# A hybrid decoder layer on one core: attention pieces a group later, psw in float32r, wider matmuls at the head of up, the last normalisation on VectorE

## The chip, the cores and the metric

The kernel runs on one core of one Trainium2 chip. The metric is the device time of one execution in microseconds (us). The core's engines are TensorE (PE in the profile, with its weight loads as PEld), VectorE (DVE), ScalarE (ACT), GpSimd (POOL) and SyncE (SP), which issues the large DMAs.

## The reference

One layer of a hybrid decoder for 256 tokens of width 1024, in float32. The functions below are cut to what is computed.

```python
def hybrid_mixer(x, w_in, ...):
    proj = x @ w_in + b_in          # q_m k_m v_m o_m i_m f_m  q_b k_b v_b  g_a g_b
    q_m, k_m = split(silu(causal_dwconv(concat(q_m, k_m), conv_qk)))      # 4 taps
    h_m = mlstm_chunkwise(q_m, k_m, v_m, i_m, f_m)       # 4 heads x 256, stabilised by a running maximum
    y_a = sigmoid(o_m) * head_norm(h_m, mlstm_norm)
    y_b = moba_attention(q_b, k_b, v_b, rel_bias)        # 8 heads x 128; 256 tokens are one block: causal softmax + T5 bias
    merged = sigmoid(g_a) * (y_a @ w_branch_a) + sigmoid(g_b) * (y_b @ w_branch_b)
    return merged @ w_out

def conv_gated_mlp(x, w_up, conv_ffn, w_down):
    g, up = split(causal_dwconv(x @ w_up, conv_ffn))     # 3 taps, 2 x 2816 columns
    return (silu(g) * up) @ w_down

x = layer_norm(ALPHA * x + hybrid_mixer(x, ...), ln1_g, ln1_b)
x = layer_norm(ALPHA * x + conv_gated_mlp(x, ...), ln2_g, ln2_b)
```

## The kernel before, in words

All weights arrive as a stream of 81 chunks, each 128 partitions x 2048 float32 columns (1 MB). `chunk_order` fixes their order: four chunks o; four groups of qm, qb, km, kb, vm, vb, ga, gb; then wa and wb in turn, wo, up, and dn between the rest of up. One chunk is one step `s` of the main loop in `run`. A step emits, in this order, the element work that is due (`elem_work`, which also splits the weights of chunk s+2), the load of chunk s+5, the chunk's own matmuls (`step_...`), and then the small matmuls that hang on this step (`side_pe`). Nothing reorders this: each engine carries out its instructions as written, and waits on semaphores for the others.

Products are made in float32r from two parts. A value is split into a high part (a float32r copy, on ScalarE) and a low part (value minus copy, on VectorE); `mm3` adds high x high, high x low and low x high in three matmuls. Line 91 is the copy and 92 the subtraction of every split; lines 125, 126 and 127 are the three matmuls of every `mm3`. Some small products are made in plain float32 instead: the profile shows each as two records.

For each group g, whose first step is b (`start_g[g]`), `group_schedule` hangs the two branches on the steps b to b+8. The names in the rows are: psw, a row of the running maximum spread over all partitions (from nM); pss, the scores of the mLSTM head; psl, the logits of the two attention heads; wt, exponential weights made from psw (`el_w`); sph and spl, the parts of the weighted scores (`el_s`, `el_s2`); psn, the mLSTM output; lg, the softmax in place; pst, its transposes; pth, ptl and ptf, their parts (`el_t`); psy, the transposes of the normalised mLSTM output yt; pso, the attention output; yah, yal, ybh, ybl, the parts of both branches' outputs (`el_y`, `el_o`). `mixed[s]` sets the order of the pieces within the element work of a step. Side results lie in five PSUM banks (`ps_side`) and chunk results in three (`ps_main`); a new tile takes a bank that an older one has left, and waits until that has been read.

The first two up chunks run one half of the tokens at a time with tokens as rows, since the second half of x1 (the first layer norm's output) comes later; `ps_t` are the transposes of x1, and `aheadh`, `aheadl` the split weights of these chunks. The other up chunks give features as rows, and `up_evac` convolves and gates them into hh and hl, the left operands of dn. dn accumulates all 1024 columns of both token halves in five banks (ffn).

After the last matmul, `finish` adds the residual (`ln_part`: r, then statistics bs), aggregates them (`ln_scale`: mv, then rs = (variance + EPS) to the power -0.5 on GpSimd), and `ln2_out` normalises r and stores it. In the second token half the columns 768 to 1023 go through ScalarE and GpSimd, the others in pieces of 256 through VectorE.

Of the kernel before, what the change touches and what calls it, by code (L numbers as in the profile page):

```python
# [18 lines left out]
P = 128  # L19
# [50 lines left out]
class Kernel:  # L70
# [101 lines left out]
    def run(self):  # L172
# [75 lines left out]
        self.xfirst = mp.tile([P, P + 16], F32R, name="xfirst")[:, 16:]  # L248
# [34 lines left out]
        self.nM = mp.tile([P, S], F32, name="nM")  # L283
        g.memset(self.nM, 0.0)
# [18 lines left out]

        self.rel_bias_expand(rel, onehot)
# [13 lines left out]
        for s, (kind, i) in enumerate(self.order):  # L318
# [12 lines left out]
            if s == first["wo"]:  # L331
                self.elem_work(s)
                y_cm.__exit__(None, None, None)
                zp = ahead_cm.__enter__()
                for j in range(2):
                    self.extra[first["up"] + j] = tuple(
                        zp.tile([P, 2112], F32R, name=f"ahead{n}{j}")[:, 8:8 + 2048] for n in "hl")
# [5 lines left out]
            self.elem_work(s, [] if late or s == 8 else self.split_parts(s + 2))  # L343
            self.load(s + 5)
# [192 lines left out]
    def gates_schedule(self, bif):  # L537
# [66 lines left out]
    def group_schedule(self, g):  # L604
# [5 lines left out]
        def pe_m():  # L610

            psw = self.ps_side([P, S], f"psw{g}")
            nc.tensor.matmul(psw, self.ident[:, g:g + 1].to_broadcast([P, P]), self.nM, start=True, stop=True)
            st["psw"] = psw

        def pe_s():
            qh, ql = self.hl["qm"]
            kh, kl = self.hl["km"]
            pss = self.ps_side([P, 2, S], f"pss{g}")

            for k in range(2):
                nc.tensor.matmul(pss[:, 0, P:], self.cv["km"][:, k, P:], self.cv["qm"][:, k, P:],
                                 start=k == 0, stop=k == 1)
            for k in range(2):
                self.mm3(pss[:, 1, :], kh[:, k, 0:P], kl[:, k, 0:P], qh[:, k, :], ql[:, k, :], k == 0, k == 1)
            st["pss"] = pss
# [89 lines left out]
        def pe_l(i):  # L716
            qh, ql, qf = self.qb
            kh, kl = self.hl["kb"]
            ps = self.ps_side([P, 2, S], f"psl{g}_{i}")

            nc.tensor.matmul(ps[:, 0, 0:P], qf[:, i, :], self.kbf[:, i, :], start=True, stop=True)
            self.mm3(ps[:, 1, :], qh[:, i, :], ql[:, i, :], kh[:, i, :], kl[:, i, :], True, True)
            st["l", i] = ps

# [38 lines left out]
        def pe_o():  # L763
            ps = self.ps_side([P, 2, S], f"pso{g}")
            vh, vl, vf = self.vb
            for i in range(2):
                th, tl, tf = self.pt[i]
# [312 lines left out]
    def ln2_out(self, t):  # L1080
# [18 lines left out]
        if t == 1:  # L1099
            store(768, D)  # L1100
# [89 lines left out]
```

## Time and profile before

| | us |
|---|---|
| median of 3 runs | 490.73 (490.67 to 490.86) |
| the profiled execution's own time | 490.16 |
| its span | 488.4 |
| TensorE busy | 477.0 (98%) |
| VectorE busy | 369.3 (76%) |
| ScalarE busy | 286.2 (59%) |
| GpSimd busy | 30.6 (6%) |

The mean granted clock of TensorE was 0.994. Times in rows count from the span's start. A row of the timeline gives the start, the duration, the engine, the line, the operation, the output and inputs by their names, shapes, and how many equal instructions it merges; in brackets stands how long the engine was idle before it, and what ended that.

### The profile page before, as it was taken

The page shows a single profiled execution, that of the slowest core. Times are in us where ns is not written, and L with a number is a line of the kernel's source. Part 1 is how long each engine was busy: PE and PEld are TensorE (multiplying, and loading weights), DVE is VectorE, ACT ScalarE, POOL GpSimd, SP SyncE. Part 2 cuts the span into 40 slices and gives each one's busy share as a digit, 9 for nine tenths or more (in the row PEclk, how much of TensorE's full clock was granted, in tenths as well). Part 3 has the DMA queues.
Part 4 walks back from the last instruction along what each step waited for, and adds up shares of the span by engine and source line. Part 5 has one row for each costly group of instructions (what it writes and reads, how often), then busy time and mean ns, then how long its engine had stood idle before and what let it go on. Part 6 is the DMA issues. An engine that isn't in the chain of part 4 may idle for free.

```text
span 488.4 us, 9811 instructions
## 1 busy us (share of the span) xinstructions
PE 477.0 (98%) x4070; PEld 470.0 (96%) x4070; DVE 369.3 (76%) x659; ACT 286.2 (59%) x476; POOL 30.6 (6%) x46
## 2 busy tenths in 40 slices
PE   8999999999999999999999999999999999999992
PEld 4999999999999999999999999999999999999992
DVE  4967995788588858886677788988668766876886
ACT  5857767495658666856655622767456545654620
POOL 0600011001100110001000001000000000000001
PEclk9999999999999999999999999999999999999997
DMA  8984565555555645543964491827465556454202
GB/s 281 376 299 122 210 196 205 178 180 188 181 191 174 189 160 197 201 150 116 368 231 172 174 344 42 302 89 258 173 236 165 205 173 224 176 204 173 87 2 86
DMA packets 17886, 93.77 MB, mean 192 GB/s; under 512 B 4497, under 2 KB 4889, under 8 KB 7857
## 3 DMA queue, kind: packets, MB, share of 16 engines
q1 hardware_dynamic: 13682, 87.08, 50.1%
q0 software_dynamic: 4160, 6.07, 4.1%
q8 instruction: 32, 0.52, 0.4%
q14 instruction: 12, 0.10, 0.1%
HBM read 92.05 MB, written 2.63 MB: 194 GB/s over the span
## 4 chain that ended last, share of the span: by engine, by line
PE 97%; DMA 1%; DVE 1%; SPq 0%; ACT 0%; issue 0%; POOL 0%; POOLq 0%
PE ps_up L127 8%; PE ps_up L125 8%; PE ps_up L126 8%; PE ffn L127 4%; PE ffn L126 4%; PE ffn L125 4%; PE ps_vm L125 2%; PE ps_qm L125 2%; PE ps_vm L126 2%; PE ps_vm L127 2%; PE ps_ga L125 2%; PE ps_ga L127 2%; PE ps_vb L125 2%; PE ps_vb L126 2%; PE ps_vb L127 2%; PE ps_ga L126 2%
## 5 line engine op out<-in xcount | busy, mean ns | idle before, releaser
L92 DVE TENSOR_TENSOR wl<-raw,wh 128x1024 fp32r<-128x1024 f32 (+1 forms) x162 | 187.7, 1199 | 25.3 <-ACT wh L91 25.2
L91 ACT CAST wh<-raw 128x1024 fp32r<-128x1024 f32 (+1 forms) x162 | 158.4, 1030 | 8.6 <-DMA raw<-in_wst_dram 5.9
L127 PE MATMUL ps_up<-x1h,wl 128*128 128x256 f32 x320 | 88.5, 277 | 0.0
L126 PE MATMUL ps_up<-x1l,wh 128*128 128x256 f32 x320 | 88.5, 276 | 0.0
L125 PE MATMUL ps_up<-x1h,wh 128*128 128x256 f32 x319 | 88.3, 277 | 0.0
L126 PEld LDWEIGHTS ps_up<-x1l,wh 128*128 128x128 f32 x320 | 60.2, 188 | 0.0
L127 PEld LDWEIGHTS ps_up<-x1h,wl 128*128 128x128 f32 x320 | 60.1, 188 | 0.0
L125 PEld LDWEIGHTS ps_up<-x1h,wh 128*128 128x128 f32 x319 | 59.9, 188 | 0.0
L1020 DVE SCALAR_TENSOR_TENSOR cu<-ps_up,vec,cu 128x255 f32<-128x255 f32 (+1 forms) x80 | 33.1, 476 | 23.1 <-ACT cu L1016 23.0
L127 PE MATMUL ffn<-wh,hl 128*128 128x256 f32 (+1 forms) x170 | 47.7, 281 | 0.0
L126 PE MATMUL ffn<-wl,hh 128*128 128x256 f32 (+1 forms) x170 | 47.7, 281 | 0.0
L125 PE MATMUL ffn<-wh,hh 128*128 128x256 f32 (+1 forms) x170 | 47.7, 281 | 0.0
L91 ACT CAST hh<-cu 128x256 fp32r<-128x256 f32 x22 | 8.9, 407 | 42.9 <-DVE cu L1028 42.9
L126 PEld LDWEIGHTS ffn<-wl,hh 128*128 128x128 f32 x170 | 32.0, 188 | 0.3
L125 PEld LDWEIGHTS ffn<-wh,hh 128*128 128x128 f32 x170 | 31.9, 188 | 0.3
L127 PEld LDWEIGHTS ffn<-wh,hl 128*128 128x128 f32 x170 | 31.9, 188 | 0.3
L1016 ACT ACTIVATE cu<-ps_up,vec 128x256 f32<-128x256 f32 x40 | 16.7, 469 | 25.7 <-PE ps_up L127 25.7
L125 PE MATMUL ps_gb<-xth,wh 128*128 128x256 f32 x64 | 18.0, 282 | 0.0
L126 PE MATMUL ps_vm<-wl,xth 128*128 128x256 f32 x64 | 17.9, 280 | 0.0
L127 PE MATMUL ps_vm<-wh,xtl 128*128 128x256 f32 x64 | 17.9, 280 | 0.0
L927 POOL TENSOR_TENSOR rs<-rs,mhalf 128x1 f32<-128x1 f32 x4 | 2.7, 666 | 242.4 <-DVE rs L926 242.4
L125 PE MATMUL mix<-wh,mgh 128*128 128x256 f32 x64 | 17.8, 279 | 0.0
(295 smaller groups left out, 1441.7 us busy)
## 6 DMA issues: line engine op xcount, KB each, us to landing
raw<-in_wst_dram SPq DMA_DIRECT2D x78, 1024.0 KB, 4.9
raw<-in_wst_dram SPq DMA_DIRECT2D x5, 512.0 KB, 8.0
lnrow<-in_rows_dram POOLq DMA_DIRECT2D x4, 512.0 KB, 6.8
band<-table POOLq DMA_DIRECT2D x4, 384.0 KB, 12.2
toe<-band POOLq DMA_DIRECT2D x4, 256.0 KB, 4.4
xtok<-in_x_dram POOLq DMA_DIRECT2D x1, 1024.0 KB, 7.7
out_dram<-r SPq DMA_DIRECT2D x3, 256.0 KB, 2.0
raw<-in_wst_dram SPq DMA_DIRECT2D x2, 256.0 KB, 3.8
```

Of the source, the lines that this page charges most:

```text
L91: self.nc.scalar.copy(wh, raw)
L92: self.nc.vector.tensor_sub(wl, raw, wh.bitcast(F32))
L125: mm(ps, ah if first is None else first, bh, start=start, stop=False)
L126: mm(ps, ah, bl, start=False, stop=False)
L127: mm(ps, al, bh, start=False, stop=stop)
L927: nc.gpsimd.tensor_tensor(st["rs"], st["rs"], self.mhalf[:, 0:1], op=ALU.pow)
L1016: act.activation(cu[:, j, :], ps[:, j, :], AF.Copy, scale=tap(2, j))
L1020: v.scalar_tensor_tensor(cu[:, j, o:], ps[:, j, :S - o], tap(t, j), cu[:, j, o:], op0=ALU.mult, op1=ALU.add)
```

## The change

- `psw` is made from nM as float32r: rows 0 to 3 hold the high part, rows 32 to 35 the low part, and a 0/1 matrix `pick` adds both in one matmul.
- Scores and logits of a group form one piece, `pe_scores`, behind step b+4, in which all plain float32 products stand together. For groups 0 to 2, `pe_t` and `pe_y` move to step b+11 and `pe_o` into the next group's `pe_scores`; `el_t` and `el_y` follow at the head of step b+12's element work, `el_o` in step b+13. `el_w` of groups 1 to 3 moves from step b+5 to the end of step b+4's element work, and their psw one step earlier.
- In group 3, `pe_o` stands ahead of `pe_y`, and `el_y` first in the element work of step b+8. The split of the chunk after wa 0 and the load of three chunks later move from step b+7 to behind that element work.
- The first two up chunks are multiplied as 512 columns (both chunks beside each other in one pair of tiles, one bank for each token half).
- dn opens with eight matmuls of 512 columns where there were nine in each of its two outer products, and inside a product both column halves follow each other for each of the three parts.
- EPS is added to the first part's statistics. `ln2_out` is one product of 1024 columns and two of 512 on VectorE, with two stores for each token half; GpSimd and ScalarE no longer take part in it, but for the power.

TensorE around the scores of group 1, before (vm is the chunk ahead, vb the one behind):

```order
L127 MATMUL ps_vm_1342<-wh_1192,xtl 128x256
L613 MATMUL psw_1392<-nM,ident 128x256
L622 MATMUL pss_1394<-cvqm,cvkm 128x128 x2
L125 MATMUL pss_1394<-qmh,kmh 128x256
...
L127 MATMUL pss_1394<-qmh,kml 128x256
L721 MATMUL psl_0_1403<-kbf,qbf 128x128
L125 MATMUL psl_0_1403<-kbh,qbh 128x256
L126 MATMUL psl_0_1403<-kbl,qbh 128x256
L127 MATMUL psl_0_1403<-kbh,qbl 128x256
L125 MATMUL ps_vb_1439<-wh_1255,xth 128x256
```

And after, from the end of kb; pst_0_1297, pst_1_1301, psy_1305 and both pso belong to group 0:

```order
L127 MATMUL ps_kb_1246<-xth,wl_1092 128x256
L622 MATMUL psw_1295<-nM,xfirst 128x256
L763 MATMUL pst_0_1297<-ident,lg_793 128x128 x3
L763 MATMUL pst_1_1301<-ident,lg_880 128x128 x3
L723 MATMUL psy_1305<-ident,yt_891 128x128 x4
L125 MATMUL ps_vm_1338<-wh_1159,xfirst 128x256
...
L781 MATMUL pso_1_1392<-pth_710,vbl 128x256
L783 MATMUL pso_0_1391<-ptf_709,vbf 128x128
L783 MATMUL pso_1_1392<-ptf_712,vbf 128x128
L635 MATMUL pss_1388<-cvqm,cvkm 128x128 x2
L637 MATMUL psl_0_1389<-kbf,qbf 128x128
L637 MATMUL psl_1_1390<-kbf,qbf 128x128
```

The transposes of the group before now stand ahead of vm, and its pso opens the block behind vm, whose float32 products follow each other.

ScalarE in the element work of that step, before:

```order
L91 CAST kmh<-cvkm 128x512
L466 ACTIVATE kbh<-ps_kb_1279,vec 128x256 x2
L468 ACTIVATE kbf<-ps_kb_1279,vec 128x128 x2
L91 CAST wh_1328<-raw_1141 128x1024 x2
L631 ACT_TABLE_LOAD
L631 ACTIVATE wt_1411<-psw_1392,gcol 128x128
```

And after:

```order
L91 CAST kmh<-cvkm 128x512
L91 CAST pth_707<-pst_0_1297 128x256
L770 COPY ptf_709<-pst_0_1297 128x128
L91 CAST pth_710<-pst_1_1301 128x256
L770 COPY ptf_712<-pst_1_1301 128x128
L730 ACTIVATE yah<-psy_1305,vec 128x256 x2
L472 ACTIVATE kbh<-ps_kb_1246,vec 128x256 x2
L474 ACTIVATE kbf<-ps_kb_1246,vec 128x128 x2
L649 ACT_TABLE_LOAD
L649 ACTIVATE wt_1328<-psw_1295,gcol 128x128
L650 ACTIVATE wt_1328<-psw_1295,gcol 128x256
L91 CAST wh_1310<-raw_1108 128x1024 x2
```

Six pieces of the group before stand ahead of kb's evacuation, and the exponentials of psw stand ahead of the casts of the next weights.

VectorE at the end of the program, before:

```order
L925 BN_AGGR mv_1_4070<-bs_1_4069 128x2
L926 TENSOR_SCALAR rs_1_4071<-mv_1_4070 128x1
L1091 TENSOR_SCALAR nmr<-mv_1_4070,rs_1_4071 128x1
L932 SCALAR_TENSOR_TENSOR r_1_4068<-r_1_4068,mv_1_4070,lnrow_4262 128x256 x2
L935 SCALAR_TENSOR_TENSOR r_1_4068<-r_1_4068,rs_1_4071,lnrow_4264 128x256 x2
L932 SCALAR_TENSOR_TENSOR r_1_4068<-r_1_4068,mv_1_4070,lnrow_4262 128x256
L935 SCALAR_TENSOR_TENSOR r_1_4068<-r_1_4068,rs_1_4071,lnrow_4264 128x256
```

And after:

```order
L950 BN_AGGR mv_1_4027<-bs_1_4026 128x2
L1116 SCALAR_TENSOR_TENSOR r_1_4025<-r_1_4025,mv_1_4027,lnrow_4220 128x1024
L1119 SCALAR_TENSOR_TENSOR r_1_4025<-r_1_4025,rs_1_4028,lnrow_4222 128x512 x2
```

The two small instructions are gone, and all 1024 columns are on VectorE, in three instructions.

The core of the diff; of the schedule tables only the lines that move pieces are shown:

```diff
-            v.tensor_scalar(self.nM[0:4, :], M, -1.0, None, op0=ALU.mult)
+            v.tensor_scalar(nM, M, -1.0, None, op0=ALU.mult)
+            nc.scalar.copy(self.nM[0:4, :], nM)
+            v.tensor_add(self.pick, self.ident[:, 0:4], self.ident[:, 32:36])
+            v.tensor_sub(self.nM[32:36, :], nM, self.nM[0:4, :].bitcast(F32))
...
-            nc.tensor.matmul(psw, self.ident[:, g:g + 1].to_broadcast([P, P]), self.nM, start=True, stop=True)
+            nc.tensor.matmul(psw, self.pick[:, g:g + 1].to_broadcast([P, P]), self.nM, start=True, stop=True)
...
+        def pe_scores():
+            pss = st["pss"] = self.ps_side([P, 2, S], f"pss{g}")
+            psl = [self.ps_side([P, 2, S], f"psl{g}_{i}") for i in range(2)]
+            if g:
+                self.grp[g - 1]["out"]()
             for k in range(2):
+                mm(pss[:, 0, P:], self.cv["km"][:, k, P:], self.cv["qm"][:, k, P:], start=k == 0, stop=k == 1)
+            for i in range(2):
+                mm(psl[i][:, 0, 0:P], self.qb[2][:, i, :], self.kbf[:, i, :], start=True, stop=True)
             for k in range(2):
                 self.mm3(pss[:, 1, :], kh[:, k, 0:P], kl[:, k, 0:P], qh[:, k, :], ql[:, k, :], k == 0, k == 1)
+            for i in range(2):
+                self.mm3(psl[i][:, 1, :], bh[:, i, :], bl[:, i, :], ch[:, i, :], cl[:, i, :], True, True)
...
+            self.mixed[b + 4] = lambda w: prev["early"] + w + [el_w]
+        self.mixed[b + 5] = lambda w: [w[0]] + ([] if g else [el_w]) + [
...
+        for i in range(2):
+            at(self.side_pe, 6 if last else 11, lambda i=i: pe_t(i))
+        if last:
+            at(self.side_pe, 7, pe_o)
+        at(self.side_pe, 7 if last else 11, pe_y)
...
+            self.mixed[b + 8] = lambda w: [el_y] + w
...
+            st["early"] = [lambda: el_t(0), lambda: el_t(1), el_y]
+            at(self.side_elem, 13, el_o)
...
             if s == first["wa"]:
                 self.elem_work(s)
+                self.split(s + 1)
+                self.load(s + 4)
...
+        if st["n"] == 0:
+            m2 = st["bs"][:, 0, 2:3]
+            v.tensor_scalar(m2, m2, D * EPS, None, op0=ALU.add)
...
-                for j in range(2):
-                    self.mm_tok(self.w[s - i + j], [self.pt_up[j][:, t, :] for t in range(2)], self.x1h, self.x1l,
-                                toks=(i,), ks=(k,))
+                self.mm3(self.pt_up[i], self.x1h[:, k, c], self.x1l[:, k, c], wh[:, :, k, :], wl[:, :, k, :], k == 0,
+                         k == KT - 1)
...
-            n = cols[1] - cols[0] if k in (0, NF - 1) else 256
+            full = ((a, b),)
+            parts = [[(c, c + 256) for c in range(a, b, 256)]] * 3
+            if k == 0:
+                parts = [full, full, parts[2] if t else full]
+            elif k == NF - 1:
+                parts = [parts[0] if t else full, full, full]
+            for i, (left, right) in enumerate(((hh, wh), (hh, wl), (hl, wh))):
+                for lo, hi in parts[i]:
+                    self.nc.tensor.matmul(ps[:, lo - a:hi - a], left, right[:, lo:hi], start=k == i == 0,
...
+        v.scalar_tensor_tensor(r, r, mv[:, 0:1], gain, op0=ALU.subtract, op1=ALU.mult)
         for h in range(2):
-            cols = [slice(x, x + 256) for x in range(h * 512, 1024 if t == 0 and h else 768 if h else 512, 256)]
-            self.ln_apply(r, st, cols)
-            store(cols[0].start, cols[-1].stop)
-        if t == 1:
-            store(768, D)
+            c = slice(h * 512, h * 512 + 512)
+            v.scalar_tensor_tensor(r[:, c], r[:, c], rs, bias[:, c], op0=ALU.mult, op1=ALU.add)
+            nc.sync.dma_start(self.out[0, t * P:(t + 1) * P, c], r[:, c])
```

More of the change, by code (lines that the diff above doesn't have):

```diff
@@ L334, in run @@
                 zp = ahead_cm.__enter__()
+                self.pair = [zp.tile([P, 4160], F32R, name="ahead" + n)[:, 24:24 + 4096] for n in "hl"]
                 for j in range(2):
-                    self.extra[first["up"] + j] = tuple(
-                        zp.tile([P, 2112], F32R, name=f"ahead{n}{j}")[:, 8:8 + 2048] for n in "hl")
+                    self.extra[first["up"] + j] = tuple(t[:, j * 2048:(j + 1) * 2048] for t in self.pair)
             if s == first["up"]:
@@ L342, in run @@
             late = s == first["up"]
-            self.elem_work(s, [] if late or s == 8 else self.split_parts(s + 2))
-            self.load(s + 5)
+            before_wa = s == first["wa"] - 1
+            self.elem_work(s, [] if late or before_wa or s == 8 else self.split_parts(s + 2))
+            if not before_wa:
+                self.load(s + 5)
             if s in (first["wo"], first["wo"] + 1):
@@ L714, in el_y @@
                                        op0=ALU.mult, op1=ALU.subtract)
[L716 to L723, printed above, removed]
         def el_l(i):
@@ L763, in pe_o @@
         def pe_o():
[L764 removed]
+            ps = st["o"] = [self.ps_side([P, S], f"pso{g}_{i}") for i in range(2)]
             vh, vl, vf = self.vb
+            mm = nc.tensor.matmul
             for i in range(2):
[L767 removed]
+                th, tl, _ = self.pt[i]
                 c = slice(i * P, (i + 1) * P)
[L769 to L774 removed]
+                mm(ps[i], vh[:, c], th, start=True, stop=False)
+                mm(ps[i], vh[:, c], tl, start=False, stop=False)
+                mm(ps[i], vl[:, c], th, start=False, stop=False)
+            for i in range(2):
+                mm(ps[i][:, P:], vf[:, i * P:(i + 1) * P], self.pt[i][2], start=False, stop=True)
+        st["out"] = pe_o
+        self.grp[g] = st
         def el_o():
@@ L925, in ln_scale @@
         v.bn_aggr(st["mv"], st["bs"][:, 0:st["n"], :].rearrange("p a b -> p (a b)"))
-        v.tensor_scalar(st["rs"], st["mv"][:, 1:2], EPS, None, op0=ALU.add)
-        nc.gpsimd.tensor_tensor(st["rs"], st["rs"], self.mhalf[:, 0:1], op=ALU.pow)
+        nc.gpsimd.tensor_tensor(st["rs"], st["mv"][:, 1:2], self.mhalf[:, 0:1], op=ALU.pow)
     def ln_apply(self, out, st, cols):
@@ L960, in step_up @@
             self.hid = {}
-            self.pt_up = [self.ps_side([P, 2, S], f"ps_up{j}") for j in range(2)]
+            self.pt_up = [self.ps_side([P, 2, S], f"ps_up0{t}") for t in range(2)]
         if i < 2:
+            wh, wl = (t.rearrange("p (j k f) -> p j k f", j=2, k=KT) for t in self.pair)
+            c = slice(i * P, (i + 1) * P)
             for k in range(KT):
@@ L979, in copy @@
             def copy():
-                for j in range(2):
-                    self.nc.scalar.copy(tu[:, j], self.pt_up[j])
+                for t in range(2):
+                    self.nc.scalar.copy(tu[:, :, t, :], self.pt_up[t])
             def back():
```

72 lines of the change are left out of this document (30 added, 42 removed).

## The prediction

> **What bounds the kernel now.** I read the page first (shares of the span, then the chain that ended last), then TensorE's instructions in order of time over one whole group and around the first up chunks, then ScalarE and VectorE around the attention steps, then everything after the last matmul. From the page, the busy line and the chain by engine:
>
> ```profile
> PE 477.0 (98%) x4070; PEld 470.0 (96%) x4070; DVE 369.3 (76%) x659; ACT 286.2 (59%) x476; POOL 30.6 (6%) x46
> PE 97%; DMA 1%; DVE 1%; SPq 0%; ACT 0%; issue 0%; POOL 0%; POOLq 0%
> ```
>
> TensorE is the bound: what shortens its stream, or the tail behind it, shortens the run; work moved on another engine counts only where TensorE would wait for it. A matmul's duration column is no price, since matmuls overlap; the price is the distance between starts. TensorE in group 1 (start, duration, instruction); left-out rows lie between:
>
> ```profile
> 97.24 0.28 PE L125 MATMUL ps_kb<-xth,wh 128*128 128x256 f32 x1
> ...
> 102.68 0.28 PE L125 MATMUL ps_vm<-wh,xfirst 128*128 128x256 f32 x1
> ...
> 108.33 0.59 PE L613 MATMUL psw<-nM,ident 128*128 128x256 f32 x2
> 108.76 0.61 PE L622 MATMUL pss<-cvqm,cvkm 128*128 128x128 f32 x4
> ...
> 110.50 0.28 PE L125 MATMUL ps_vb<-wh,xth 128*128 128x256 f32 x1
> ...
> 115.95 0.38 PE L721 MATMUL psl<-kbf,qbf 128*128 128x128 f32 x2
> ...
> 117.61 0.28 PE L125 MATMUL ps_ga<-xth,wh 128*128 128x256 f32 x1
> ...
> 123.08 0.82 PE L754 MATMUL pst<-ident,lg 128*128 128x128 f32 x6
> 123.65 0.37 PE L125 MATMUL ps_gb<-xth,wh 128*128 128x256 f32 x1
> 123.86 0.28 PE L126 MATMUL ps_gb<-xtl,wh 128*128 128x256 f32 x1
> ...
> 129.20 0.60 PE L705 MATMUL psy<-ident,yt 128*128 128x128 f32 x4
> ...
> 130.79 0.28 PE L125 MATMUL ps_qm<-xth,wh 128*128 128x256 f32 x1
> ```
>
> A reader should see four prices here. The 48 matmuls of kb take 102.68 - 97.24 = 5.44 us, so 0.113 us each; this is the quick spacing. The 48 of vm take 5.65, 0.118 each, although they are of the same size: a second, slower spacing. psw, a full-precision float32 product of 256 columns, is two records and takes 108.76 - 108.33 = 0.43 us, so 0.1075 us for a float32 pass of 128 columns. And six float32 transposes with the first gb matmul take 123.86 - 123.08 = 0.78; less 0.113 and 6 x 0.1075 = 0.645 this leaves 0.02 us for one break, from float32 back to float32r.
>
> **The change, part by part.**
>
> *psw in float32r.* Its 0.43 us becomes one matmul of 256 columns, 0.113 to 0.118. Four groups: 4 x 0.313 = 1.25 us gained, on the path. What it costs (a copy on ScalarE, an add and a subtraction on VectorE, once, on small tiles in step b+2 of group 0) is first asked for by the gate transposes behind kb, a step later, and by psw two steps later; I cost it at nothing. Its cover is step kb, 5.4 us.
>
> *Grouping the float32 pieces.* Before, each group has seven breaks: behind pss, psl_0, psl_1, pst, psy and twice in pso, 28 in all. After, there are nine: one in the scores of each group (4), one behind pst and psy for groups 0 to 2 (3), and two in group 3. 19 fewer x 0.02 = 0.4 us. Bounds: 0, if a break costs nothing where float32r matmuls follow anyway, to 0.5.
>
> *The spacing behind a moved piece.* vm of groups 1 to 3 follows kb directly before, and runs slow; now it follows the transposes, as gb does, which took 129.20 - 123.86 = 5.34 for its last 47 matmuls, 0.114 each. If vm becomes quick, 3 x 0.2 = 0.6 us are gained; if vb and ga, now entered from other neighbours, become slow in those groups, 6 x 0.2 = 1.2 are lost. I take +0.3, nearer to the gb row, and keep both ends.
>
> *Up's first chunks.* The rows around the second token half, and the spacing of 512 columns in the first steps:
>
> ```profile
> 12.21 0.39 PE L159 MATMUL ps_o0b<-wh,xth 128*128 128x512 f32 x1
> 12.44 0.39 PE L159 MATMUL ps_o<-wh,xtl 128*128 128x512 f32 x1
> ...
> 296.77 0.28 PE L125 MATMUL ps_up<-aheadh,x1h 128*128 128x256 f32 x1
> ...
> 301.73 0.60 PE L947 MATMUL ps_t<-ident,x 128*128 128x128 f32 x4
> ...
> 303.42 0.28 PE L126 MATMUL ps_up<-aheadl,x1h 128*128 128x256 f32 x1
> 303.73 0.39 PE L127 MATMUL ps_up<-aheadh,x1l 128*128 128x256 f32 x1
> ```
>
> 512 columns take 0.23 us, twice 0.113: by this row a wider matmul saves nothing in itself. The trace weighs against a rule here. The Trainium skill ("TensorE: Matmul & The Clock Gate", "Wait — 56ns, not 53.3ns?") gives each warm matmul a fixed 2.5 ns beside its columns; by that, 48 matmuls fewer would be an estimated 0.12 us gained. But the 42 matmuls before 301.73 stand 0.118 apart, so 96 x 0.0045 = 0.4 us could go if the wide ones take the quick spacing; bounds 0 to 0.4, I take 0.1, since what follows directly keeps its spacing in most rows above. The third matmul of the second half needs the low part of x1 and waits: 303.73 - 303.42 = 0.31 instead of 0.12. With 512 columns it stands third behind two of 0.23, so it is due 0.23 later and the wait of about 0.2 goes; 0.2 gained. Late next is nothing I can name there.
>
> *Down's first and last products.* Two matmuls of 512 columns fewer and four of 256 more, and the order of the halves inside a product is swapped: nothing, as long as the spacing stays quick; the other case is a rival.
>
> *What must now be ready earlier.* In step b+4 ScalarE and VectorE do el_t twice and el_y for the group before, then the evacuation of kb, then el_w, all ahead of the two weight casts, and TensorE asks for them behind vm. psl_1 takes the bank that psw held, so it waits for el_w. Rows of before with those durations (ScalarE but for the first):
>
> ```profile
> 103.88 0.68 DVE L92 TENSOR_TENSOR kml<-cvkm,kmh 128x512 fp32r<-128x512 f32 x1
> ...
> 103.61 0.83 ACT L466 ACTIVATE kbh<-ps_kb,vec 128x256 fp32r<-128x256 f32 x2
> ...
> 104.84 2.01 ACT L91 CAST wh<-raw 128x1024 fp32r<-128x1024 f32 x2
> 106.86 1.28 ACT L631 ACT_TABLE_LOAD   x1
> ...
> 109.23 0.47 ACT L632 ACTIVATE wt<-psw,gcol 128x256 f32<-128x256 f32 x1
> ...
> 123.61 0.37 ACT L91 CAST pth<-pst 128x256 fp32r<-128x256 f32 x1 [1.99 <-PE pst L754]
> 124.47 0.27 ACT L761 COPY ptf<-pst 128x128 f32<-128x128 f32 x1 [0.49 <-DVE ptl L92]
> ...
> 130.13 0.47 ACT L712 ACTIVATE yah<-psy,vec 128x256 fp32r<-128x256 f32 x1
> 131.16 0.47 ACT L712 ACTIVATE yah<-psy,vec 128x256 fp32r<-128x256 f32 x1 [0.55 <-DVE yal L713]
> ```
>
> On group 1's clock: VectorE is free at 103.88 + 0.68 = 104.56, so the first ptf starts about 105.05; the second head 1.0 later; el_y's two yah 1.03 apart, the second at about 107.3; kb's evacuation (104.84 - 103.61 = 1.23) until 108.9; the table 1.28 and wt about 0.75: el_w ends near 110.9. TensorE reaches psl_1 at 102.68 + 0.12 + 10 transposes (1.09) + vm 5.65 + six float32r (0.70) + ten float32 passes (1.08) = 111.3. The margin is 0.4 us, where before nothing was near. Behind it the casts and subtractions for the next weights, then vm's evacuation, el_l, el_s and spl run some 4 us later than now, and spl has under 1 us left before psn. In group 3 the same squeeze comes at the output: weights of chunk wb 0 are now split after el_y and el_o, with casts (2.0) and subtractions ending about when TensorE needs them. The loads that were behind that split start a step (5.4 us) later, against a landing of about 5 us and three steps of lead. I charge 0.2 us for waits, between 0 and 1.5 (0.5 in three groups).
>
> *The tail.* VectorE but where marked, behind the last matmul; the first rows are two durations used below; last, the stores (number, issue, landing):
>
> ```profile
> 473.53 0.87 DVE L932 SCALAR_TENSOR_TENSOR r<-r,mv,lnrow 128x256 f32<-128x256 f32 x2
> 473.76 0.67 POOL L927 TENSOR_TENSOR rs<-rs,mhalf 128x1 f32<-128x1 f32 x1 [170.56 <-DVE rs L926]
> ...
> 476.85 0.68 DVE L919 SCALAR_TENSOR_TENSOR r<-x,ffn 128x512 f32<-128x512 f32 x1
> ...
> 479.49 0.42 DVE L919 SCALAR_TENSOR_TENSOR r<-x,ffn 128x256 f32<-128x256 f32 x1 [0.44 <-PE ffn L127]
> ...
> 480.40 0.24 DVE L925 BATCH_NORM_AGGREGATE mv<-bs 128x2 f32<-128x18 f32 x1
> ...
> 480.97 0.54 POOL L927 TENSOR_TENSOR rs<-rs,mhalf 128x1 f32<-128x1 f32 x1 [6.54 <-DVE rs L926]
> ...
> 482.48 1.05 POOL L1093 TENSOR_TENSOR r<-r,lnrow 128x256 f32<-128x256 f32 x1 [0.96 <-ACT r L1092]
> ...
> 483.74 0.94 DVE L932 SCALAR_TENSOR_TENSOR r<-r,mv,lnrow 128x256 f32<-128x256 f32 x1
> 484.71 0.48 DVE L935 SCALAR_TENSOR_TENSOR r<-r,rs,lnrow 128x256 f32<-128x256 f32 x1
> ...
> L1085 SPq DMA_DIRECT2D out_dram<-r x5: 332/343/432, 475.5 to 485.6; - x5
> DMA to landing us min/median/max: 1.9/2.0/2.0
> ```
>
> After: the aggregate ends at 480.64 and, with EPS already in the statistics, POOL's power follows at once (about 480.8 to 481.35), while VectorE starts the 1024-column product at 480.67. From 256 columns at 0.48 and a slope of 0.26 per 256 (0.68 - 0.42), it takes 1.26, until 481.95; the two halves of 512 take 0.74, 0.65 apart, so the last store is issued at about 483.4 instead of 485.6: 2.2 us gained. Both store sizes land in 2.0 us, so the larger last store costs nothing. One thing can eat into it: VectorE reads two SBUF tensors while POOL wants its own two columns. In the rows POOL's power took 0.67 beside VectorE and 0.54 alone, and VectorE's 256 columns took 0.94 beside POOL's product against 0.48. From 0.13 (the row of the same power) to its whole wait (the power only starting at 481.95 and ending 482.4, so 0.45 lost), I take 0.2: tail 2.0 gained.
>
> Sum: 1.25 + 0.4 + 0.3 + 0.1 + 0.2 + 2.0 - 0.2 = 4.05 us. The profiled execution took 490.16 (span 488.4 and 1.8 around it), so 486.1 by its own time; the median of the runs shown, 490.73, lies 0.57 higher, and I put the same gain there: 486.7.
>
> **The rivals.**
> - *The power waits out the whole product.* For it: POOL's product at 482.48 and VectorE's beside it never ran together at full rate. Price 0.45 instead of 0.2: 486.95. The Trainium skill ("SBUF — State Buffer", "Who interferes with whom") says that a Vector instruction with two SBUF inputs contends with a GpSimd instruction that reads SBUF, and that whoever issues first keeps the shared pair; the 0.94 row agrees, while the 0.67 row shows only 0.13 of it.
> - *The attention pieces come late.* My margins of 0.4 at psl_1 and under 1 at spl are made of some twenty durations; half a microsecond late at each in three groups is up to 2 us with the charge replaced: 487.2 to 489.5, middle 488.3. Against it: VectorE's and ScalarE's idle shares of 24% and 41%.
> - *The other side: the slow spacing settles in up and down.* About 960 matmuls in up behind the first two chunks and 500 in down run at 0.1133 now; down's inner order is new. At 0.118 down alone costs 2.3 us (489.0); with up 6.9, so 493. It decides from 4.05 / 0.0046 = 880 slow matmuls. Against it: before, the slow first chunks and the wide down products are both followed by quick ones.
> - *Better than forecast:* vm and the wide up chunks all quick, no waits: 0.3 + 0.3 + 0.2 less, 485.9, with the power unhindered 485.7.
>
> **How the numbers follow.** Chances: forecast 0.44; the power's full wait 0.26; attention late 0.18, of which 0.02 beyond 489.75; slow spacing 0.07, of which 0.05 slower than before and 0.02 about the same; better 0.05. A measurement of this kernel tells about 0.2%, 1 us, from no change. Faster than 489.75: 0.44 + 0.26 + 0.16 + 0.05 = 0.91; same 0.04; slower 0.05. The range goes from 485.2, the better case with half a microsecond for what the breaks and spacings may still give, to 489.2, most of the late case; left out is about 0.12.
>
> **What would show it.** psw as one record, 0.12 before the next start, four times; no wait of TensorE on wt, spl, pth or kbl above 0.3 us; vm of groups 1 to 3 at 5.45; the first up matmuls 0.23 apart with no gap at the second half; nothing on POOL behind the power, the last store issued within 4.1 us of the last matmul (6.1 now). The prediction is wrong if TensorE waits in steps b+4 or b+5 by over 1 us a group, or if up and down are spaced 0.118.

## The result, and the profile after

The changed kernel took 487.47 us (median of four runs, 487.25 to 487.74), the one before 490.7 (490.6 to 490.86): 0.9932 of its time, 95% interval 0.992 to 0.9943, so 3.2 us faster. The forecast was 486.7. The profiled execution took 487.25, with a span of 485.5 and the granted clock of before, 0.994. Its busy line and chain by engine:

```profile
PE 474.6 (98%) x4020; PEld 464.8 (96%) x4020; DVE 368.0 (76%) x652; ACT 285.3 (59%) x476; POOL 30.5 (6%) x44
PE 94%; DMA 2%; DVE 1%; SPq 1%; issue 0%; POOLq 0%; DVEq 0%; ACT 0%
```

TensorE lost 2.4 us of busy time and is still the bound. In the chain TensorE has 94% where it had 97%, and DMA has 2%, 10 us, where 1% stood. The stages tell more than the page. The table is worked out from the two traces, from the start of one matmul to the start of another: the head goes from the span's start to the first qm matmul, a group from its first qm to the next group's (group 3 to the first wa), "up 0 to 3" are the four up chunks ahead of down's first product, "up and down" is the rest of both, and "tail" goes from the last matmul to the issue of the last store.

| us | head | group 0 | 1 | 2 | 3 | wa, wb | wo | up 0 to 3 | up and down | tail | to the end |
|---|---|---|---|---|---|---|---|---|---|---|---|
| before | 29.72 | 51.20 | 49.87 | 49.89 | 49.89 | 43.53 | 22.68 | 24.48 | 157.92 | 6.43 | 2.84 |
| after | 31.68 | 48.38 | 49.29 | 49.29 | 51.45 | 43.63 | 22.68 | 23.71 | 157.75 | 4.67 | 2.99 |

The four groups together gain 2.44 us (some of their work has moved a group later, hence the uneven shares), up 0.77, up and down 0.17, the tail 1.76; wa and wb lose 0.10 and the store's landing 0.15. That is 4.9 us gained behind the head. The head gave back 1.96, though no instruction of it was changed.

TensorE in group 1, which answers to the first timeline of before:

```profile
101.82 0.28 PE L622 MATMUL psw<-nM,xfirst 128*128 128x256 f32 x1
101.94 0.82 PE L763 MATMUL pst<-ident,lg 128*128 128x128 f32 x6
102.59 0.60 PE L723 MATMUL psy<-ident,yt 128*128 128x128 f32 x4
102.95 0.37 PE L125 MATMUL ps_vm<-wh,xfirst 128*128 128x256 f32 x1
103.16 0.28 PE L126 MATMUL ps_vm<-wl,xth 128*128 128x256 f32 x1
...
108.49 0.28 PE L779 MATMUL pso<-pth,vbh 128*128 128x256 f32 x1
...
109.64 0.61 PE L635 MATMUL pss<-cvqm,cvkm 128*128 128x128 f32 x4
110.09 0.61 PE L637 MATMUL psl<-kbf,qbf 128*128 128x128 f32 x4
```

psw is one record of 0.12 (it was two, 0.43). pst and psy stand back to back, and vm takes 108.49 - 102.95 = 5.54 instead of 5.65: its first matmul, behind the float32 transposes, takes 0.21 until the next start, the other 47 stand (108.49 - 103.16) / 47 = 0.113 apart, the quick spacing. No start is late by a wait; TensorE's list of waits is empty behind the head. The element work that had to be ready earlier, ScalarE on the same clock:

```profile
108.05 1.28 ACT L649 ACT_TABLE_LOAD   x1
109.34 0.37 ACT L649 ACTIVATE wt<-psw,gcol 128x128 f32<-128x128 f32 x1
109.61 0.47 ACT L650 ACTIVATE wt<-psw,gcol 128x256 f32<-128x256 f32 x1
```

wt ends at 110.08. The first two records of psl are psl_0, so psl_1 is due at 110.09 + 0.22 = 110.31, where it does start: the margin was 0.2 us.

TensorE in up's first chunks, at their start and at the second token half:

```profile
296.41 0.40 PE L125 MATMUL ps_up<-aheadh,x1h 128*128 128x512 f32 x1
296.64 0.40 PE L126 MATMUL ps_up<-aheadl,x1h 128*128 128x512 f32 x1
...
303.24 0.47 PE L127 MATMUL ps_up<-aheadh,x1l 128*128 128x512 f32 x1
303.55 0.40 PE L125 MATMUL ps_up<-aheadh,x1h 128*128 128x512 f32 x1
```

The tail, VectorE, POOL and SP's stores, with the row of the stores' size and landing time last:

```profile
479.10 0.24 DVE L950 BATCH_NORM_AGGREGATE mv<-bs 128x2 f32<-128x18 f32 x1
479.38 1.28 DVE L1116 SCALAR_TENSOR_TENSOR r<-r,mv,lnrow 128x1024 f32<-128x1024 f32 x1
479.49 1.58 POOL L951 TENSOR_TENSOR rs<-mv,mhalf 128x1 f32<-128x1 f32 x1 [5.27 <-DVE mv L950]
481.10 1.41 DVE L1119 SCALAR_TENSOR_TENSOR r<-r,rs,lnrow 128x512 f32<-128x512 f32 x2 [0.44 <-POOL rs L951]
481.88 1.00 SPq L1120 DMA_DIRECT2D out_dram<-r  x2
out_dram<-r SPq DMA_DIRECT2D x4, 256.0 KB, 2.0
```

The wide up matmuls stand 0.23 apart. The gap at the second half, 0.2 beyond the spacing, has shrunk to 303.55 - 303.24 - 0.23 = 0.08. In the tail POOL's power of one column, which took 0.54 in the last row of before, takes 1.58: it starts 0.11 behind VectorE's product and ends 0.41 behind its end (481.07 against 480.66).

### The profile page after: what moved, and what is told of

The parts are those of the page before. It is cut to its first block, busy times and chain, and to the rows that moved or that the text cites. A ratio compares the mean times of both kernels' runs of the same rounds, so it can differ in the third digit from the quotient of the medians.

```text
span 485.5 us, 9705 instructions
## 1 busy us (share of the span) xinstructions
PE 474.6 (98%) x4020; PEld 464.8 (96%) x4020; DVE 368.0 (76%) x652; ACT 285.3 (59%) x476; POOL 30.5 (6%) x44
## 4 chain that ended last, share of the span: by engine, by line
PE 94%; DMA 2%; DVE 1%; SPq 1%; issue 0%; POOLq 0%; DVEq 0%; ACT 0%
PE ffn L1081 12%; PE ps_up L126 8%; PE ps_up L127 8%; PE ps_up L125 8%; DMA raw<-in_wst_dram 2%; PE ps_vm L125 2%; PE ps_qm L125 2%; PE ps_vb L126 2%; PE ps_vb L127 2%; PE ps_vb L125 2%; PE mix L125 2%; PE ps_wa L126 2%; PE ps_wb L126 2%; PE ps_ga L126 2%; PE ps_qm L126 1%; PE ps_vm L126 1%
## 5 line engine op out<-in xcount | busy, mean ns | idle before, releaser
L1081 PE MATMUL ffn<-wh,hh 128*128 128x256 f32 (+1 forms) x171 | 37.9, 279 | 0.0
L1081 PE MATMUL ffn<-wh,hl 128*128 128x256 f32 (+1 forms) x171 | 37.9, 280 | 0.0
L1081 PE MATMUL ffn<-wl,hh 128*128 128x256 f32 (+1 forms) x170 | 37.9, 280 | 0.0
L1081 PEld LDWEIGHTS ffn<-wh,hh 128*128 128x128 f32 x171 | 27.7, 188 | 0.3
L1081 PEld LDWEIGHTS ffn<-wh,hl 128*128 128x128 f32 x171 | 27.6, 188 | 0.3
L1081 PEld LDWEIGHTS ffn<-wl,hh 128*128 128x128 f32 x170 | 27.4, 188 | 0.2
L951 POOL TENSOR_TENSOR rs<-mv,mhalf 128x1 f32<-128x1 f32 x4 | 4.3, 1072 | 241.2 <-DVE mv L950 241.2
L125 PE MATMUL ps_qm<-xth,wh 128*128 128x256 f32 x64 | 17.8, 278 | 0.0
L125 PE MATMUL ps_qb<-xth,wh 128*128 128x256 f32 x64 | 17.8, 277 | 0.0
L125 PE MATMUL ps_wa<-yah,wh 128*128 128x256 f32 x64 | 17.8, 277 | 0.0
```

What stands on the lines that cost most here:

```text
L125: mm(ps, ah if first is None else first, bh, start=start, stop=False)
L951: nc.gpsimd.tensor_tensor(st["rs"], st["mv"][:, 1:2], self.mhalf[:, 0:1], op=ALU.pow)
L1081: self.nc.tensor.matmul(ps[:, lo - a:hi - a], left, right[:, lo:hi], start=k == i == 0, stop=k == NF - 1 and i == 2)
```

## The experiments

All twelve, with what the next sections rest on. The second column is the number of matmul records on the page; GB/s is what the DMA engines moved from 2 to 4 us; the stages are those of the table above; "own" is the profiled execution, to which they belong.

| kernel | PE records | GB/s, 2 to 4 us | head | up 0 to 3 | up and down | tail | own | median |
|---|---|---|---|---|---|---|---|---|
| before | 4070 | 246 | 29.72 | 24.48 | 157.92 | 6.43 | 490.16 | 490.7 |
| before, again | 4070 | 270 | 30.19 | 24.48 | 157.92 | 6.44 | 490.63 | 490.63 |
| new tail only | 4070 | 272 | 30.41 | 24.48 | 157.92 | 4.67 | 489.23 | 489.21 |
| up as before | 4068 | 294 | 30.18 | 24.54 | 157.75 | 4.67 | 486.57 | 486.77 |
| idle matmuls ahead of down | 4068 | 275 | 29.82 | 23.71 | 170.57 | 4.67 | 498.22 | 498.44 |
| idle matmuls behind all | 4068 | 274 | 30.80 | 23.71 | 157.75 | 4.28 | 486.05 | 486.39 |
| after | 4020 | 159 | 31.68 | 23.71 | 157.75 | 4.67 | 487.25 | 487.47 |
| after, again | 4020 | 166 | 31.69 | 23.71 | 157.75 | 4.67 | 487.27 | 487.27 |
| product in halves | 4020 | 175 | 31.96 | 23.71 | 157.75 | 4.27 | 487.13 | 487.04 |
| tail as before | 4020 | 166 | 31.18 | 23.71 | 157.75 | 6.43 | 488.38 | 488.57 |
| psw in float32 | 4024 | 178 | 32.19 | 23.71 | 157.75 | 4.67 | 489.06 | 488.96 |
| el_w later | 4020 | 168 | 32.24 | 23.71 | 157.75 | 4.67 | 493.41 | 493.01 |
| wide up only | 4022 | 164 | 31.37 | 23.69 | 163.62 | 6.43 | 496.74 | 497.31 |
| 96 memsets on POOL | 4020 | 170 | 31.58 | 23.71 | 157.75 | 4.37 | 486.84 | 487.08 |

**Both kernels again, and the tail's product in two halves.** The first two runs are the kernels unchanged. The edit of the third:

```diff
-        v.scalar_tensor_tensor(r, r, mv[:, 0:1], gain, op0=ALU.subtract, op1=ALU.mult)
+        for h in range(2):
+            c = slice(h * 512, h * 512 + 512)
+            v.scalar_tensor_tensor(r[:, c], r[:, c], mv[:, 0:1], gain[:, c], op0=ALU.subtract, op1=ALU.mult)
```

> The kernel before, unchanged, for a second look at its head (the time from the span's start to the first ps_qm matmul: 29.72 us in its first profile, 31.68 in the profile after). Theory 1, the head varies from run to run with the landing of the first loads and the change has no part in it: the head differs from 29.72 by some tenths to 2 us, and what follows it (29.72 to 488.4, so 458.7 us) is the same within 0.2. Theory 2, the later head belongs to the changed program: the head is again 29.7 within 0.2.

> The kernel after, unchanged. Theory 1: the head is not again 31.68 but somewhere between 29.5 and 32, the rest 453.8 within 0.2 (485.5 less 31.68), and the ratio to before stays at 0.9932 within 0.001, since before's heads vary as well. Theory 2: the head is 31.7 within 0.2.

> After, with the first product of the last normalisation (128x1024) in two halves of 512 columns on VectorE. Theory A, POOL's power waits for the running VectorE instruction and not for the work as a whole (in the profile after it took 1.58 us beside the 1024 columns and ended 0.41 behind them): the power now ends about 0.4 behind the first half, at some 1.1 us after the aggregate's end instead of 1.73, the second half ends at about 1.45, and the last store is issued 0.25 to 0.3 us earlier against the last matmul (4.67 from its start to the store in the profile after). Theory B, the power is slow for another reason (its operand is a column of mv instead of rs): it still takes 1.5 us and the last store comes 0 to 0.1 later. In the time 0.3 us is at the edge of what can be told.

Both repeats came out as the first time, to 0.2 us (after again: 0.9931, 0.9918 to 0.9943). The head of before came 0.47 later than the first time, that of after to 0.01 the same: before's head moves by some tenths, and 1.5 us or more stay between the two kernels. The halves gave 487.04 (0.9924, 0.9912 to 0.9937). Its tail, VectorE and POOL:

```profile
479.65 1.42 DVE L1118 SCALAR_TENSOR_TENSOR r<-r,mv,lnrow 128x512 f32<-128x512 f32 x2
479.76 1.05 POOL L951 TENSOR_TENSOR rs<-mv,mhalf 128x1 f32<-128x1 f32 x1 [5.80 <-DVE mv L950]
480.98 1.41 DVE L1121 SCALAR_TENSOR_TENSOR r<-r,rs,lnrow 128x512 f32<-128x512 f32 x2
```

The power now takes 1.05 instead of 1.58: it ends at 480.81, 0.41 after the end of the first half (479.65 + 0.75 = 480.40), and the second half covers it. It follows the VectorE instruction that is running when it is issued, not the whole of VectorE's work. The tail is 0.40 shorter; the whole run, by its median, only 0.2 to 0.4, which the intervals do not tell from nothing; its head, 0.3 longer here, took a part.

**One part undone or done alone.** The tail of before in the changed kernel (statistics, power and output); the tail alone in the kernel before; psw and nM in float32 as before; up's first chunks as before (256 columns, one bank for each chunk), everything else changed; and el_w two places later in its step:

```diff
-            self.mixed[b + 4] = lambda w: prev["early"] + w + [el_w]
+            self.mixed[b + 4] = lambda w: prev["early"] + w + [None, None, el_w]
```

> After, with the statistics, the power and the output of both layer norms as before (EPS added behind the aggregate, columns 768 to 1023 over ScalarE and POOL, pieces of 256, three last stores). If the tail is worth what the two profiles show, 6.43 us from the last matmul's start to the last store before against 4.67 after, this is 1.75 us slower than after: 489.2, ratio to before 0.9968. By the prediction's forecast (2.0) 489.5; if the tail is not on the path, as after, 487.5.

> Before, with only the statistics, the power and the output of both layer norms as after. By the profiles the tail is worth 1.76 us (6.43 us from the last matmul's start to the last store, 4.67 after) less 0.15 that the end behind the store grew: 1.6 us faster than before, 489.0. On the head (first ps_qm matmul; 29.72 and 30.19 in two profiles of before; 31.68, 31.69, 31.97 and 31.18 in four of after and its variants): no instruction of the head differs in any of these. Theory 2a, the head goes with the program as a whole, with whatever its image changes about the first loads: it is anywhere between 29.5 and 32. Theory 2b, it goes with the attention or weight-load part: it is 29.7 to 30.2 here.

The tail goes both ways by the same amount: 6.43 with the old one in the changed kernel, 4.67 with the new one in the old kernel, 1.76 us. Medians 488.57 (0.9958, 0.9942 to 0.9973) and 489.21 (0.9961, 0.9922 to 0.9999). The first is 0.6 below the 489.2 that was expected; its head is 0.5 earlier than the changed kernel's.

> After, with psw in plain float32 from nM as before (one mult into rows 0 to 3, the identity as the spreading operand). My term: 4 x 0.313 = 1.25 us slower, 488.5; in the profile each inner group (49.29 us) becomes 0.31 longer, 49.60, and of the 0.58 that an inner group gained 0.27 stay with the grouping. Rival: the float32 psw adds one break less than it saves, since the transposes behind it are float32 too: 0.29 each.

The groups grew by 0.32, 0.33, 0.33 and 0.33, 1.31 together. TensorE at psw:

```profile
102.65 0.59 PE L619 MATMUL psw<-nM,ident 128*128 128x256 f32 x2
103.08 0.82 PE L760 MATMUL pst<-ident,lg 128*128 128x128 f32 x6
```

0.43 again instead of 0.12: the float32r product is worth what its rows said. The median, 488.96, is 0.5 above the 488.5 expected; by as much the head was later in this profile.

> After, with el_w of groups 1 to 3 behind the two weight casts of its step instead of ahead of them. In the profile after, el_w ends at 110.08 and psl_1, which takes its bank, starts at about 110.31: no wait. Behind two casts (2.0 us) el_w ends at 112.1: TensorE waits 1.7 to 1.8 us in each of three groups, 5.2 slower, 492.6. If psl_1 does not wait for el_w, or if the wait is made good later in the group, it stays within 0.5 of after.

The waits of TensorE, and its rows at psl in group 1:

```profile
PE psl L637 <- ACT wt L650: 4.6, 3, 1.5
```

```profile
110.65 0.39 PE L637 MATMUL psl<-kbf,qbf 128*128 128x128 f32 x2
112.55 0.49 PE L637 MATMUL psl<-kbf,qbf 128*128 128x128 f32 x2 [1.52 <-ACT wt L650]
```

psl_1 waits three times, up to 1.5 us, for wt to leave the bank of psw; groups 1 to 3 grew by 1.79, 2.02 and 1.79, and the kernel ended at 493.01 (1.0028, 0.999 to 1.0067), the whole gain gone. Two casts ahead of el_w cost 2.0 us of ScalarE, and all but the margin of 0.2 reached TensorE. The wait the prediction feared is there, at the place it named; the changed order just avoids it.

> After, with the first two up chunks in 256 columns as before (tiles and their places as after). From the first up matmul to the first of down took 24.48 us before and 23.71 after. Theory P, the wide matmuls themselves bring it (the wait at the second half and the spacing): 24.48, 0.77 us slower, 488.2. Theory Q, half of it is the place of the operands, which stays: 24.1, 0.4 slower.

Up 0 to 3 grew by 0.83, a little more than theory P said, and yet the median fell to 486.77 (0.9914, 0.9889 to 0.9938; the interval overlaps that of the changed kernel). Its head is 1.5 us shorter than that of the changed kernel. The run does not bring the stage of before back piece by piece: its first two chunks took 12.66 us (12.30 before, 11.93 after), while up 2 and 3 took 11.88 (12.18 before, 11.77 after), because the last 71 of their 96 matmuls, behind up's transposes, stand 0.113 apart although these first chunks are not wide.

**What sets the head.** After these eight, the head was early (29.7 to 30.4) in the four profiles with 256-column first chunks of up and late (31.2 to 32.2) in the six others. Two views show it: TensorE's window from 2 to 4 us, whose last two columns are the share and rate of the DMA engines, and the first cast of weights on ScalarE. In the kernel before they read:

```profile
2.00:4.00 2.00, 2.00 (x6) 1.00 0.98 246
```

```profile
3.98 0.62 ACT L91 CAST wh<-raw 128x512 fp32r<-128x512 f32 x1 [0.40 <-DMA raw<-in_wst_dram]
```

The same two in the changed kernel:

```profile
2.00:4.00 2.00, 2.00 (x6) 1.00 1.00 159
```

```profile
6.45 0.62 ACT L91 CAST wh<-raw 128x512 fp32r<-128x512 f32 x1 [2.86 <-DMA raw<-in_wst_dram]
```

And the window in the run with up as before:

```profile
2.00:4.00 2.00, 2.00 (x6) 1.00 0.97 294
```

The DMA engines are as busy in all three, but after moves 159 GB/s where before moves 246: the same loads, issued at the same time (1.22 us), land 2.5 us later. Three runs ask what in the program does it: the wide chunks alone in the kernel before; 48 idle matmuls ahead of down's first product, whose sums they leave alone; and 96 memsets of one column on POOL, during up 3, the fourth of up's 22 chunks.

```diff
+            if k == 0 and t == 0 and a == 0:
+                for _ in range(48):
+                    self.nc.tensor.matmul(ps[:, 0:64], hh, wh[:, 0:64], start=True, stop=True)
```

> The kernel before with one part of the change alone: up's first two chunks in 512 columns, both chunks' weights in one pair of tiles. The open question is the head, the time from the start of the span to the first matmul of qm: 29.7 to 30.4 us in the four programs seen so far with 256-column first chunks (48 matmuls and 48 weight loads more on TensorE), 31.2 to 32.2 in the six with 512-column ones, although the instructions of the head are the same in all. Theory H (the late head goes with the programs that have the wide chunks, or are shorter by them): head 31.2 to 32.2, up 23.7 instead of 24.5, so 490.7 + 1.5 - 0.8 = 491.4, no faster or slightly slower than before. Theory G (the late head goes with the moved attention pieces or with chance): head 30, time 490.7 - 0.8 = 489.9.

> The changed kernel with 48 idle matmuls of 64 columns (and their weight loads) put before down's first product, which overwrites what they leave. They do no work; they only make TensorE's program as long as that of before. Theory L (the late head goes with the length of TensorE's program): head 30.2 instead of 31.7, against 1.5 to 3 us for the 48 matmuls, where they stand: total 487.3 to 489. Theory U (it goes with the wide chunks themselves or with something else than that length): head 31.2 to 32.2, total 489 to 490.5.

> The changed kernel with 96 one-column memsets of a tile that nothing reads, on POOL, during up's last chunk, where POOL has nothing to do: the same number of instructions added as in the run with the idle matmuls, but on another engine, off the path. Theory T (the late head goes with the length of the whole program): head 30.2 instead of 31.7, time 485.8. Theory L (with the length of TensorE's program) and theory U (with the wide chunks): head 31.2 to 32.2, time 487.3, as the changed kernel.

The heads were 31.37, 29.82 and 31.58: late with the shorter TensorE program even in the otherwise old kernel, early when idle matmuls fill it up, late when the filling is on POOL. So far theory L. But the first two ended at 497.31 (1.0133, 1.0118 to 1.0148) and 498.44 (1.0159, 1.013 to 1.0188), which no theory had. The place is up and down: 163.62 and 170.57 instead of 157.75. TensorE around down's first product, in the kernel before:

```profile
320.90 0.28 PE L125 MATMUL ps_up<-x1h,wh 128*128 128x256 f32 x1
321.02 0.28 PE L126 MATMUL ps_up<-x1l,wh 128*128 128x256 f32 x1
...
321.25 0.39 PE L125 MATMUL ffn<-wh,hh 128*128 128x512 f32 x1
...
324.26 0.28 PE L127 MATMUL ffn<-wh,hl 128*128 128x256 f32 x1
...
325.51 0.28 PE L126 MATMUL ffn<-wl,hh 128*128 128x256 f32 x1
```

In the changed kernel:

```profile
319.78 0.28 PE L125 MATMUL ps_up<-x1h,wh 128*128 128x256 f32 x1
...
320.12 0.39 PE L1081 MATMUL ffn<-wh,hh 128*128 128x512 f32 x1
...
324.93 0.28 PE L1081 MATMUL ffn<-wh,hh 128*128 128x256 f32 x1
...
325.50 0.28 PE L1081 MATMUL ffn<-wh,hl 128*128 128x256 f32 x1
```

And with the wide chunks alone in the kernel before:

```profile
321.76 0.28 PE L125 MATMUL ps_up<-x1h,wh 128*128 128x256 f32 x1
...
322.10 0.39 PE L125 MATMUL ffn<-wh,hh 128*128 128x512 f32 x1
...
324.31 0.28 PE L126 MATMUL ffn<-wl,hh 128*128 128x256 f32 x1
...
325.49 0.28 PE L127 MATMUL ffn<-wh,hl 128*128 128x256 f32 x1
```

In the first, up comes at 0.118 (321.02 - 320.90, which two digits show as 0.12; the twelve matmuls before stand 0.117 to 0.119 apart), and behind nine matmuls of 512 columns the spacing is (325.51 - 324.26) / 11 = 0.1136. In the second, up comes at 0.113, (320.12 - 319.78) / 3, and stays there behind eight: (325.50 - 324.93) / 5 = 0.114. In the third up comes at 0.113, as in the second, down opens with nine, as in the first, and the spacing becomes (325.49 - 324.31) / 10 = 0.118, which lasts until shortly before the end: each of the 26 stretches of 48 matmuls between has 0.1178. These 1,248 matmuls at 0.0045 more are 5.6 of the 5.9 us. This is the third rival of the prediction, run. Whether it is the nine instead of eight, the other order inside a product or the last products that decides, no run separates. Nor does the order of before always end in the quick spacing, it seems: in the series with the new tail alone and with psw, up or el_w undone, 5 of 31 executions of the kernel before took 496.2 to 496.7 us instead of 490.7, the same 5.9 us, and 1 of 10 with the new tail alone took 494.2. None of these was traced, so the cause is not shown there.

The run with idle matmuls ahead of down lost 12.8 us there, in three parts: 5.4 are the 48 matmuls, some 1.5 a slower clock behind them, and the rest again a spacing of 0.1178, behind eight wide matmuls this time. TensorE's windows from the end of the idle ones on (busy time, matmuls, granted clock, DMA share, GB/s):

```profile
321.00:323.60 2.60, 2.60 (x25) 0.97 0.89 340
323.60:326.80 3.20, 3.20 (x10) 0.50 0.08 31
```

The expectation had 1.5 to 3 us for them; that run can only speak for the head. The memsets left the time as it was, 487.08 (0.9931, 0.9914 to 0.9948).

**The last run** puts the idle matmuls where they move nothing, behind the last useful one, and takes the product in halves along:

```diff
     def finish(self):
+        ps, (hh, wh) = self.ps_side([P, S], "pad_ps"), self.last
+        for _ in range(48):
+            self.nc.tensor.matmul(ps[:, 0:64], hh, wh[:, 0:64], start=True, stop=True)
```

> The changed kernel with the tail's first product in two halves (as in the run that split it) and 48 idle matmuls of 64 columns behind TensorE's last useful matmul, into a bank of their own that nothing reads; they run while VectorE and the stores finish, so they cost nothing, and no matmul ahead of them is moved. Theory L (the late head goes with a shorter TensorE program): head 30.0 instead of 31.7, tail 4.27, groups, up and down as in the changed kernel, so 487.3 - 1.7 - 0.4 = 485.3 us, below both kernels. If the early head of the run with the idle matmuls ahead of down was chance: head 31.7, time 486.9.

486.39 us (485.94 to 486.77; 0.9909, 0.9892 to 0.9925), the shortest of all medians here but 1.1 above the 485.3 expected; its ratio's interval still overlaps that of the changed kernel, 0.9918 to 0.9943. Groups, up and down are those of the changed kernel, the tail is 4.28. The window from 2 to 4 us, and then the first qm matmul, in this run:

```profile
2.00:4.00 2.00, 2.00 (x6) 1.00 1.02 274
```

```profile
30.80 0.39 PE L125 MATMUL ps_qm<-xth,wh 128*128 128x256 f32 x1
```

The rate is that of the early heads; the head of 30.80 lies between (30.0 was expected; the fourth load landed at 9.50 us here, at 8.33 to 9.14 in the other five with the higher rate and at 9.84 to 10.30 in the eight with the lower). Over fourteen profiles the rate parts cleanly: 246 to 294 GB/s in the six with 4068 to 4070 records on TensorE, 159 to 178 in the eight with 4020 to 4024. That this rate goes with the length of TensorE's program is shown for these two lengths, by filling it at two places and by filling POOL's without effect. The heads go with it: 29.72 to 30.80 in the six, 31.18 to 32.24 in the eight. One more row of the pages parts the same way: queue q8, instruction, has 32 packets in the six and 31 in the eight. But in none of the fourteen traces does a packet of an instruction queue start between 0.1 and 21 us, so by these traces it is not fetching beside the first loads that slows them. Why the length matters, by where the program and the arrays lie in memory for example, no run here tells.

## Why the prediction was right or wrong

The time was 0.8 us above the forecast and well inside the range. The sum's steps behind the head gave more than it said, and the head, which was in no step, took back nearly two.

- *psw in float32r*: 1.25 forecast, 1.31 measured by the run in float32. Right, and the copy, addition and subtraction cost nothing that shows.
- *Grouping, the spacing behind moved pieces, and the charge for waits*: 0.4 + 0.3 - 0.2 = 0.5 forecast; the groups' 2.44 less 1.31 leave 1.13. The two traces split it. From the second to the last matmul, vm of groups 1 to 3 takes 5.34 instead of 5.54: it turned quick, 0.20 each, the upper end of the term, and only the longer first matmul hides half of it. ga of group 0, which the prediction did not name, turned quick too (0.20), and vb and ga of groups 1 to 3, which were feared, stayed quick. All chunks together give 0.9; so about 0.2 is left for the breaks, where 0.4 was forecast. The spacing is the mis-sized term here. No wait came, so the charge was not due.
- *The margin*: 0.4 at psl_1 was forecast, 0.2 is in the rows. The second rival stayed away by that much: with el_w two casts later it came true, at 5.6 us and not 2.
- *Up's first chunks*: 0.3 forecast, 0.77 measured between the two kernels (0.83 against the run with up as before). The first two chunks took 0.37 less, near the forecast. The rest, 0.41, is up 2 and 3, which came at 0.113 instead of 0.118; the prediction counted the first two chunks alone. That the wide matmuls bring this is not shown, since in the run with up as before up 3 was quick without them.
- *Down's first and last products*: costed at nothing, with the case of another spacing left to a rival. In the changed kernel it is 0.17 gained together with up. But nothing was the wrong word for it: behind quick up chunks, the order of before would have cost some 5.9, by the run with the wide chunks alone. Its argument was that before both slow chunks and wide products were followed by quick ones. In the traces nine wide matmuls behind slow ones left quick ones, nine behind quick ones left slow ones, and eight behind quick ones kept the quick, except behind the idle matmuls; so that argument did not carry over to quick up chunks. The price in the rival, 6.9 with all of up and down, was near; the condition was missing. The changed kernel with the old order of down alone was not run; the run with the wide chunks alone has the old order, but also old attention pieces and an old tail, whose stages are those of before to 0.01.
- *The tail*: 2.0 forecast, 1.76 measured less 0.15 in the landing of the larger last store, which the prediction had put at nothing. The first rival is what happened: the power waits out the product, 1.58 against 0.54, and its price (0.45 instead of 0.2) gives just the 1.75 that the tail shows. The prediction took the row of 0.67 for a wait of only 0.13. It was a whole wait too, for a product of only 256 columns: the first of the two in its row ended at 474.01 and the power at 474.43, 0.42 later, as it ends 0.41 behind 1024 columns and 0.41 behind 512. The Trainium skill ("SBUF — State Buffer", "SBUF: two separate sides") has it so, that of a VectorE instruction with two SBUF inputs and a GpSimd instruction that reads SBUF the one that starts first keeps the shared ports for its whole instruction, and that the other blocks fully. The trace agrees as far as the power waits. What decides the order when both start almost together is not in the records. In the run with memsets the power starts 0.05 behind the product in both token halves; in the first it waits, in the second it does not, and the tail is 0.30 shorter:

```profile
472.40 1.28 DVE L1120 SCALAR_TENSOR_TENSOR r<-r,mv,lnrow 128x1024 f32<-128x1024 f32 x1
472.45 1.66 POOL L951 TENSOR_TENSOR rs<-mv,mhalf 128x1 f32<-128x1 f32 x1 [156.80 <-DVE mv L950]
...
479.27 1.31 DVE L1120 SCALAR_TENSOR_TENSOR r<-r,mv,lnrow 128x1024 f32<-128x1024 f32 x1
479.32 0.54 POOL L951 TENSOR_TENSOR rs<-mv,mhalf 128x1 f32<-128x1 f32 x1 [5.21 <-DVE mv L950]
480.69 1.42 DVE L1123 SCALAR_TENSOR_TENSOR r<-r,rs,lnrow 128x512 f32<-128x512 f32 x2
```

In all runs together, 22 powers start 0.05 behind a product: 20 take 0.54 to 0.57, beside a product only 0.02 to 0.04 longer, and two wait (0.87 and 1.66). All that start 0.11 or more behind wait. By the records the product starts first in all 22, and where the power does not wait the product does not wait out the power's 0.54 either; so the rule does not describe that side. That the memsets bring the shorter tail of their run is not shown, and it may be luck.

- *The head*: in no term. The sum was made against one profiled execution of before whose head was the shortest of all, 29.72, and took for granted that what is not edited keeps its time. By the runs, 48 matmuls fewer on TensorE made the head 1.5 us longer (30.18 to 31.68 between the run with up as before and the changed kernel), more than the 0.83 that the wide chunks earn. Without that, the forecast would have been too high by 0.8: 490.16 less 4.9 is 485.3 by its own time, where it had 486.1. The agreement to 0.8 is in part two errors of opposite sign.

## What to carry to other kernels

Make the sum by stages and compare by stages: a total that fits can hide terms at less than half their size and a loss that no term had. Two identical matmuls can be spaced 0.113 or 0.118, and over a thousand behind a changed order or width went over to the other spacing; so after any edit of widths or order in a stream that TensorE bounds, read the spacing of what follows, all the way to the end. And when an engine off the path is to work beside VectorE for a moment, split VectorE's long instruction: in halves it made the tail 0.40 shorter.

## What the runs showed of the hardware that was not expected

- The rate at which the first loads move, 159 to 178 or 246 to 294 GB/s at DMA shares of 0.91 to 1.08 and 0.96 to 1.02, went with the number of instructions in TensorE's program, which differ by some 96 (matmuls with their weight loads) hundreds of microseconds later.
- The idle matmuls have 64 columns and took about as long as those of 256: 48 in 5.76 us, 0.12 each, beside weight loads of 0.119 each in the same window (run with idle matmuls behind all); ahead of down they stood 0.112 apart:

```profile
476.99 5.73 PEld L1128 LDWEIGHTS pad_ps<-wh,hh 128*128 128x128 f32 x48
477.10 5.76 PE L1128 MATMUL pad_ps<-wh,hh 128*128 128x64 f32 x48
```

Each of these matmuls has a weight load of its own, though the weight is the same; 64 columns instead of 256 gain next to nothing here.
- Ahead of down, 48 such matmuls in a row were followed by 3.2 us at a granted clock of 0.50, with 512 columns 0.43 apart instead of 0.23, though TensorE counts as busy throughout.
